# Second mixer of a hybrid decoder trunk: decay and exponential loads with four buffers on ScalarE's queue, decay arithmetic ordered behind the second chunk back

## The chip, the core and the metric

The kernel runs on one core of a Trainium2 chip. A core has five engines that work side by side, each through its own queue in order: TensorE (PE, matmuls and transposes), VectorE (DVE), ScalarE (ACT), GpSimd (POOL) and SyncE (SP, which here only issues loads and stores). They wait for each other by semaphores. Sixteen DMA engines move data between memory (HBM) and the on-chip buffers. The metric is the time of one execution on the device in microseconds (us), as the median of several runs.

## What is computed

A trunk of two layers over 1024 tokens of width 1024, in float32. Layer 0 mixes with an mLSTM and a retention group, layer 1 with a Mamba-2 state-space mixer (SSD); each is followed by a squared-ReLU MLP. The change is in the SSD mixer only. Its core, cut to what matters:

```python
def ssd_chunked(x, dt, a, bm, cm):
    # h_t = exp(dt_t a) h_{t-1} + dt_t x_t B_t^T ;  y_t = h_t C_t, in chunks of 128 tokens
    cs = jnp.cumsum(dt * a.reshape(ng, rep), axis=2)
    seg = jnp.exp(jnp.where(mask, cs[:, :, :, None] - cs[:, :, None, :], -jnp.inf))
    cb = jnp.einsum('bctgn,bcsgn->bctsg', cm, bm)
    m = cb[..., None] * seg * dt[:, :, None]
    y_intra = jnp.einsum('bctsgr,bcsgrp->bctgrp', m, x)
    to_end = jnp.exp(cs[:, :, -1:] - cs) * dt
    states = jnp.einsum('bclgn,bclgr,bclgrp->bcgrpn', bm, to_end, x)
    ...
    y_inter = jnp.einsum('bctgn,bcgrpn->bctgrp', cm, h_prev) * jnp.exp(cs)[..., None]
    return (y_intra + y_inter).reshape(bsz, seq, nh, hp)
```

There are 32 heads in 8 groups of 4 heads; a group shares its B and C (`bm`, `cm`).

## The kernel before

Activations stay on chip for the whole trunk. A projection matrix is kept as a high and a low half (`whi`, `wlo`), and so is the input (`uh`, `ul`); each tile of a projection is a run of 24 matmuls of 128x512 (`proj_in`, L136).

The second mixer is `ssd`. A helper, `ssd_dt`, first works out the cumulated decay `cs` and its exponential `ecs` for all heads and writes both to memory as `cs_d` and `ecs_d`, one row a head. Then a loop over the 8 groups does, for each:

- four projections with two halves of 512 tokens each (B, C, two of x), each followed by a causal convolution: ScalarE copies the product into `xr`, VectorE adds three shifted taps (L784), ScalarE takes a tanh into `th` (L788), VectorE makes the SiLU of it (L789);
- per half, `cb` = C times B for its four chunks (matmuls `cbp`, L811, times a mask, L815);
- per chunk of 128 tokens, the decay tile `cb4` for 4 heads: a load broadcasts a piece of `cs_d` to all 128 partitions (L822), four activations subtract the token's own value (L826, one a head), one takes the exponential (L833), VectorE multiplies it with `cb` (L834);
- in the same chunk on TensorE: three transposes `tr` (L839), the product `yp` within the chunk from `cb4` and `xd` (L848), the product with the carried state (L853), and the new contribution to the state, `ds_`, from `xw` and `bn` (L868). `xd` and `xw` are VectorE's scaled copies of the transposed x (L842, L862); `bn` is ScalarE's plain copy of the transposed B (L866);
- the state update (`sst`: L875 on GpSimd, L880 on VectorE; for chunk 0 the copy L873 on ScalarE), and the output: `eh` (the broadcast `ecs`) times the state product (L882), the skip term (L884) and their sum (L893);
- the gate: two projections `sz` (L903, L904), norm, and the output projection (`proj_out`, L180).

In the trace and in the order, `cb` followed by a number is the tile `cb4`; its loads are written `cb<-cs_d`. In that notation `ds__12166` is a buffer of `ds_` by its number.

The order in which each engine gets its instructions is set by the tile framework's scheduler from the program order and its dependencies; it fills TensorE's queue between the small products of a chunk with matmuls of the following projections (`mmin`, L136). Within an engine nothing overtakes. A tile with `bufs=n` has n buffers in turn, and an instruction that writes a buffer waits until the last reader of its former content is done. `cb4` has two buffers, `eh` one of a whole half, `th` two, `xr` three. Every load is issued by SP (`nc.sync`), in one line with the weights.

Of the kernel before, what the change touches and what calls it, by code (L numbers as in the profile page):

```python
# [7 lines left out]
F32 = mybir.dt.float32  # L8
F32R = mybir.dt.float32r
AF = mybir.ActivationFunctionType  # L10
ALU = mybir.AluOpType

P = 128
# [4 lines left out]
HALF = 512  # L18
# [5 lines left out]
class Trunk:  # L24
# [704 lines left out]
    def ssd(self, w_in, conv_w, conv_b, dt_bias, a_log, d_skip, norm_w, w_out, mask):  # L729
        nc, tc = self.nc, self.tc  # L730
        with ExitStack() as ctx:
            one = ctx.enter_context(tc.tile_pool(name="ss1", bufs=1))
            two = ctx.enter_context(tc.tile_pool(name="ss2", bufs=2))
# [27 lines left out]
            nat, cs_d, ecs_d, dec, by_token = self.ssd_dt(one, w_in, dt_bias, a_log)  # L761


            for g in range(8):
                conv = []
                for j in (2, 3, 0, 1):
                    jt = (g * 2, g * 2 + 1, 16 + g, 24 + g)[j]
                    w = self.split_in(self.load_in(w_in, 2048 + jt * P))
                    outs = []
                    prev = None  # L770
                    for half in range(2):
                        ps = self.proj_in(w, half)
                        t = self.half_tile(half, f"sact{half}")
                        xr = two.tile([P, HALF + 3], F32, name="xr", tag="xr", bufs=3)
                        if half == 0:
                            nc.gpsimd.memset(xr[:, 0:3], 0.0)
                        else:
                            nc.gpsimd.tensor_copy(xr[:, 0:3], prev[:, HALF : HALF + 3])
                        nc.scalar.copy(xr[:, 3 : 3 + HALF], ps)
                        nc.scalar.activation(  # L780
                            t, ps, AF.Identity, scale=cw[:, 3, jt : jt + 1], bias=cw[:, 4, jt : jt + 1]
                        )
                        for k in range(3):
                            nc.vector.scalar_tensor_tensor(  # L784
                                t, xr[:, k : k + HALF], cw[:, k, jt : jt + 1], t, op0=ALU.mult, op1=ALU.add
                            )
                        th = two.tile([P, HALF], F32, name="th", tag="th", bufs=2)
                        nc.scalar.activation(th, t, AF.Tanh)  # L788
                        nc.vector.scalar_tensor_tensor(t, th, 1.0, t, op0=ALU.add, op1=ALU.mult)  # L789
                        outs.append(t)  # L790
                        prev = xr
                    conv.append(outs)
# [3 lines left out]
                hs = slice(g * 4, g * 4 + 4)  # L796
                state = None
                for half in range(2):
                    o = half * HALF
                    eh = two.tile([P, 2, HALF], F32, name="eh", tag="eh", bufs=1)  # L800
                    for tl in range(2):
                        for j in range(2):
                            nc.sync.dma_start(
                                eh[j * 64 : (j + 1) * 64, tl],
                                ecs_d[g * 4 + tl * 2 + j, o : o + HALF].partition_broadcast(64),
                            )

                    cbp = self.sc.tile([P, CPH, P], F32, name="cbp", tag="sc")
                    for cc in range(CPH):
                        s = slice(cc * P, (cc + 1) * P)  # L810
# [3 lines left out]
                    cb = two.tile([P, CPH, P], F32, name="cb", tag="cb", bufs=1)  # L814
                    nc.vector.tensor_mul(cb, cbp, m01.unsqueeze(1).broadcast_to([P, CPH, P]))  # L815
                    y = (x0[half], x1[half])
                    for cc in range(CPH):
                        c = half * CPH + cc
                        s = slice(cc * P, (cc + 1) * P)
                        par, q = c % 2, c // 2  # L820
                        cb4 = two.tile([P, 4, P], F32, name="cb4", tag="cb4", bufs=2)
                        nc.sync.dma_start(  # L822
                            cb4, cs_d[hs, c * P : (c + 1) * P].partition_broadcast(P)
                        )
                        for h in range(4):
                            nc.scalar.activation(  # L826
                                cb4[:, h],
                                cb4[:, h],
                                AF.Relu,
                                scale=-1.0,  # L830
                                bias=nat[:, 2, par, g * 4 + h, q : q + 1],
                            )
                        nc.scalar.activation(cb4, cb4, AF.Exp, scale=-1.0)  # L833
                        nc.vector.tensor_mul(  # L834
                            cb4, cb4, cb[:, cc].unsqueeze(1).broadcast_to([P, 4, P])
                        )
                        tr = self.sc.tile([P, 4, P], F32, name="tr", tag="sc")
                        for j, src in enumerate((x0, x1, bT)):
                            nc.tensor.transpose(tr[:, j], src[half][:, s], self.ident)  # L839
                        xn = tr[:, 0:2].rearrange("p a (h d) -> p (a h) d", h=2)  # L840
                        xd = two.tile([P, 4, 64], F32, name="xd", tag="xd")
                        nc.vector.tensor_mul(  # L842
                            xd, xn, nat[:, 0, par, hs, q : q + 1].broadcast_to([P, 4, 64])
                        )
                        yp = self.sc.tile([P, 4, P], F32, name="yp", tag="sc")
                        for h in range(4):
                            r = slice((h % 2) * 64, (h % 2) * 64 + 64)
                            nc.tensor.matmul(  # L848
                                yp[r, h // 2], xd[:, h], cb4[:, h], start=True, stop=True
                            )  # L850
                        if c > 0:
                            for tl in range(2):
                                nc.tensor.matmul(  # L853
                                    yp[:, 2 + tl],
                                    state[:, tl * P : (tl + 1) * P],
                                    cT[half][:, s],
                                    start=True,
                                    stop=True,
                                )
                        if c < NCH - 1:  # L860
                            xw = two.tile([P, 4, 64], F32, name="xw", tag="xw")
                            nc.vector.tensor_mul(  # L862
                                xw, xn, nat[:, 1, par, hs, q : q + 1].broadcast_to([P, 4, 64])
                            )
                            bn = two.tile([P, P], F32, name="bn", tag="bn")
                            nc.scalar.copy(bn, tr[:, 2])  # L866
                            ds_ = self.sc.tile([P, HALF], F32, name="ds_", tag="sc")
                            nc.tensor.matmul(  # L868
                                ds_[:, 0:256], bn, xw.rearrange("p h d -> p (h d)"), start=True, stop=True
                            )  # L870
                            new = two.tile([P, 256], F32, name="sst", tag="sst")
                            if c == 0:
                                nc.scalar.copy(new, ds_[:, 0:256])  # L873
                            else:
                                nc.gpsimd.tensor_mul(  # L875
                                    new.rearrange("p (h d) -> p h d", h=4),
                                    state.rearrange("p (h d) -> p h d", h=4),
                                    dec[:, hs, c : c + 1].broadcast_to([P, 4, 64]),
                                )
                                nc.vector.tensor_add(new, new, ds_[:, 0:256])  # L880
                        if c > 0:
                            nc.vector.tensor_mul(eh[:, :, s], eh[:, :, s], yp[:, 2:4])  # L882
                        for tl in range(2):
                            nc.vector.scalar_tensor_tensor(  # L884
                                y[tl][:, s],
                                y[tl][:, s],
                                dsk[:, g * 2 + tl : g * 2 + tl + 1],
                                yp[:, tl],
                                op0=ALU.mult,
                                op1=ALU.add,  # L890
                            )
                            if c > 0:
                                nc.vector.tensor_add(y[tl][:, s], y[tl][:, s], eh[:, tl, s])  # L893
                        if c < NCH - 1:
                            state = new
                zs = []
# [214 lines left out]
```

## Time and profile before

| | |
|---|---|
| median of 3 runs | 2788.24 us (2787.37 to 2789.55) |
| the profiled execution, its own time | 2785.3 us |
| its span, first to last instruction | 2783.5 us |
| TensorE busy, share of the span | 2706.2 us, 97% |
| VectorE busy | 1702.9 us, 61% |
| ScalarE busy | 928.1 us, 33% |
| GpSimd busy | 526.6 us, 19% |
| DMA engines, share by the queue of the loads | 19.4% |
| mean granted TensorE clock | 0.993 |

The profile is of one execution. Busy time of TensorE is the time in which a matmul was in its pipeline. The second mixer lies between 1176 and 2085 us of the span.

### The profile page before, as it was taken

Reading aid. Unit: us, or ns where it says so; the run is one execution under the profiler, and the core shown is the slowest. Engines: PE = TensorE matmul, PEld = TensorE weight load, DVE = VectorE, ACT = ScalarE, POOL = GpSimd, SP = SyncE. Lnnn points to the kernel's source line nnn. Section 1 sums busy time; section 2 is a strip of 40 time slices with the busy share of each in tenths; the row PEclk is TensorE's granted clock in tenths of the full one; section 3 lists DMA queues with packets and bytes.
Section 4 is the critical chain, followed back from the end, with each engine's and each line's share of the span. In section 5 each row is a group of like instructions: output and inputs, shape, how many; then the busy total and the mean of one; then the engine's idle time right before and its main releaser. Section 6 shows DMA issues by size and latency. Waiting matters only on the chain.

```text
span 2783.5 us, 32858 instructions
## 1 busy us (share of the span) xinstructions
PE 2706.2 (97%) x12973; PEld 2195.3 (79%) x12973; DVE 1702.9 (61%) x2790; ACT 928.1 (33%) x1515; POOL 526.6 (19%) x526
## 2 busy tenths in 40 slices
PE   8999999999999999899999999999999999999997
PEld 7788788888888888677777787777878888888885
DVE  5663537654466644776766667667676456654457
ACT  5232224222222222453434434344343222222223
POOL 1010111422222322200000000000013222332223
PEclk9999999999999999899999999999999999999998
DMA  4111112110111110132312222222121112110111
GB/s 159 39 62 46 54 54 68 54 41 27 61 61 61 54 38 25 43 84 61 76 51 72 69 61 69 57 72 71 59 54 63 52 61 61 61 38 24 60 38 61
DMA packets 199050, 161.46 MB, mean 58 GB/s; under 512 B 8952, under 2 KB 177840, under 8 KB 198768
## 3 DMA queue, kind: packets, MB, share of 16 engines
q1 hardware_dynamic: 198896, 159.36, 19.4%
q8 instruction: 102, 1.67, 0.2%
q14 instruction: 52, 0.43, 0.1%
HBM read 154.68 MB, written 4.62 MB: 57 GB/s over the span
## 4 chain that ended last, share of the span: by engine, by line
PE 90%; DMA 4%; ACT 2%; DVE 2%; POOL 1%; issue 0%; SPq 0%; DVEq 0%; ACTq 0%; POOLq 0%
PE mmin L136 49%; PE mmout L260 22%; PE mmout L180 9%; DMA cb<-cs_d 4%; PE mmnat L152 3%; PE yp L848 1%; PE pt L223 1%; ACT cb L826 1%; POOL h L355 1%; DVE un L206 1%; PE mmin L162 1%; PE cbp L811 1%; PE av L546 0%; PE tr L839 0%; PE sp L924 0%; PE av L548 0%
## 5 line engine op out<-in xcount | busy, mean ns | idle before, releaser
L136 PE MATMUL mmin<-uh,whi 128*128 128x512 f32 (+1 forms) x2112 | 826.7, 392 | 0.3 <-ACT uh L225 0.3
L136 PE MATMUL mmin<-ul,whi 128*128 128x512 f32 (+1 forms) x2112 | 825.6, 391 | 0.0
L136 PE MATMUL mmin<-uh,wlo 128*128 128x512 f32 (+1 forms) x2112 | 823.5, 390 | 0.0
L136 PEld LDWEIGHTS mmin<-uh,whi 128*128 128x128 f32 x2112 | 397.3, 188 | 89.8 <-issue 1.2
L136 PEld LDWEIGHTS mmin<-uh,wlo 128*128 128x128 f32 x2112 | 397.4, 188 | 88.5 <-issue 0.2
L136 PEld LDWEIGHTS mmin<-ul,whi 128*128 128x128 f32 x2112 | 397.3, 188 | 86.8
L94 DVE TENSOR_TENSOR wlo<-raw,whi 128x1024 fp32r<-128x1024 f32 x240 | 309.6, 1293 | 220.5 <-ACT whi L93 214.0
L93 ACT CAST whi<-raw 128x1024 fp32r<-128x1024 f32 (+1 forms) x243 | 251.1, 1038 | 452.8 <-PE mmin L136 215.3
L260 PE MATMUL mmout<-whi,hl 128*128 128x512 f32 x896 | 353.7, 395 | 0.7 <-DVE hl L94 0.7
L260 PE MATMUL mmout<-wlo,hh 128*128 128x512 f32 x896 | 353.7, 395 | 0.0
L260 PE MATMUL mmout<-whi,hh 128*128 128x512 f32 x896 | 353.6, 395 | 0.0
L180 PE MATMUL mmout<-whi,hid 128*128 128x512 f32 x768 | 245.3, 398 | 0.7 <-ACT hid L610 0.7
L311 DVE TENSOR_TENSOR q<-q 128x512 f32<-128x512 f32 x128 | 95.2, 744 | 222.2 <-ACT q L310 222.2
L283 DVE TENSOR_TENSOR h<-h,mmout 128x512 f32<-128x512 f32 x320 | 208.6, 678 | 33.3 <-PE mmout L260 33.1
L260 PEld LDWEIGHTS mmout<-whi,hl 128*128 128x128 f32 x896 | 168.6, 188 | 41.0 <-DVE hl L94 1.1
L260 PEld LDWEIGHTS mmout<-wlo,hh 128*128 128x128 f32 x896 | 168.6, 188 | 39.9
L260 PEld LDWEIGHTS mmout<-whi,hh 128*128 128x128 f32 x896 | 168.6, 188 | 39.9
L784 DVE SCALAR_TENSOR_TENSOR sact<-xr,cw,sact 128x512 f32<-128x512 f32 x192 | 144.0, 750 | 55.3 <-ACT sact L780 51.4
L180 PEld LDWEIGHTS mmout<-whi,hid 128*128 128x128 f32 x768 | 143.4, 188 | 35.8 <-ACT hid L610 2.4
L310 ACT ACTIVATE q<-mmin 128x512 f32<-128x512 f32 x128 | 76.2, 596 | 269.8 <-PE mmin L136 269.8
L93 ACT CAST hh<-q 128x1024 fp32r<-128x1024 f32 x80 | 84.1, 1051 | 199.0 <-PE mmout L260 110.0
L180 PE MATMUL mmout<-wlo,hid 128*128 128x512 f32 x384 | 150.0, 395 | 0.0
(377 smaller groups left out, 3171.1 us busy)
## 6 DMA issues: line engine op xcount, KB each, us to landing
raw<-in_mlp_w_dram SPq DMA_DIRECT2D x64, 512.0 KB
raw<-in_mlp_w_dram SPq DMA_DIRECT2D x32, 1024.0 KB
raw<-in_ssd_w_in_dram SPq DMA_DIRECT2D x48, 512.0 KB
cb<-cs_d SPq DMA_DIRECT2D x64, 256.0 KB
raw<-in_hyb_w_in_dram SPq DMA_DIRECT2D x24, 512.0 KB
raw<-in_ssd_w_out_dram SPq DMA_DIRECT2D x16, 512.0 KB
eh<-ecs_d SPq DMA_DIRECT2D x64, 128.0 KB
h<-in_x_dram SPq DMA_DIRECT2D x8, 512.0 KB
```

The costliest lines, as they stand in the source:

```text
L93: self.nc.scalar.copy(hi, raw)
L94: self.nc.vector.tensor_sub(lo, raw, hi.bitcast(F32))
L136: self.nc.tensor.matmul(ps[:, o : o + n], a[:, k], u[:, k, s], start=(k == 0 and i == 0), stop=(k == 7 and i == 2),)
L152: self.nc.tensor.matmul(ps, u[:, k, s], a, start=(k == 0 and i == 0), stop=(k == 7 and i == 2))
L162: self.nc.tensor.matmul(ps, w[:, k], u[:, k, s], start=(k == 0 and i == 0), stop=(k == 7 and i == 1))
L180: self.nc.tensor.matmul(ps, a[:, s], w[:, n], start=(kk == 0 and i == 0), stop=(kk == 1 and i == 2))
L206: nc.vector.scalar_tensor_tensor(un[j], self.h[:, c, n], r, wb[j], op0=ALU.mult, op1=ALU.mult)
L260: nc.tensor.matmul(banks[t], a[x][:, kk, s], w[y][:, kk], start=(not more and kk == 0 and i == 0), stop=(not more and kk == 1 and i == 2), ...
L283: nc.vector.tensor_add(y, y, x[t])
L310: nc.scalar.activation(x, ps, AF.Relu)
L311: nc.vector.tensor_mul(x, x, x)
L784: nc.vector.scalar_tensor_tensor(t, xr[:, k : k + HALF], cw[:, k, jt : jt + 1], t, op0=ALU.mult, op1=ALU.add)
```

## The change

The loads of the decay tile go from SP's queue to ScalarE's, with four buffers in place of two. `eh` is loaded per chunk instead of per half: two loads of 64 KB a chunk (none for chunk 0) with four buffers, in place of four loads of 128 KB a half; these too are issued by ScalarE. The activations and the multiply that make the decay tile of a chunk are told to be issued behind two instructions of the second chunk back, its `xw` and its `bn` (`tc.issue_after`; the list `issued` starts empty in each call and runs on over halves and groups, and is an empty entry for the last chunk of a group). The tanh of the convolution writes into the first 512 columns of `xr`, so that `th` needs no memory of its own.

```diff
@@ ssd
+            issued = []
             for g in range(8):
...
-                        th = two.tile([P, HALF], F32, name="th", tag="th", bufs=2)
+                        th = xr[:, 0:HALF]
                         nc.scalar.activation(th, t, AF.Tanh)
...
                 for half in range(2):
-                    o = half * HALF
-                    eh = two.tile([P, 2, HALF], F32, name="eh", tag="eh", bufs=1)
-                    for tl in range(2):
-                        for j in range(2):
-                            nc.sync.dma_start(
-                                eh[j * 64 : (j + 1) * 64, tl],
-                                ecs_d[g * 4 + tl * 2 + j, o : o + HALF].partition_broadcast(64),
-                            )
...
-                        cb4 = two.tile([P, 4, P], F32, name="cb4", tag="cb4", bufs=2)
-                        nc.sync.dma_start(
+                        cb4 = two.tile([P, 4, P], F32, name="cb4", tag="cb4", bufs=4)
+                        nc.scalar.dma_start(
                             cb4, cs_d[hs, c * P : (c + 1) * P].partition_broadcast(P)
                         )
-                        for h in range(4):
-                            nc.scalar.activation(
...
+                        if c > 0:
+                            eh = two.tile([P, 2, P], F32, name="eh", tag="eh", bufs=4)
+                            for j in range(2):
+                                nc.scalar.dma_start(
+                                    eh[j * 64 : (j + 1) * 64],
+                                    ecs_d[hs, c * P : (c + 1) * P]
+                                    .rearrange("(a b) t -> b a t", b=2)[j]
+                                    .partition_broadcast(64),
+                                )
+                        with ExitStack() as order:
+                            for ins in issued[-2] if len(issued) >= 2 else ():
+                                order.enter_context(tc.issue_after(ins))
+                            for h in range(4):
+                                nc.scalar.activation(
+                                    cb4[:, h],
...
+                            nc.scalar.activation(cb4, cb4, AF.Exp, scale=-1.0)
+                            nc.vector.tensor_mul(
...
+                        issued.append([])
                         if c < NCH - 1:
                             xw = two.tile([P, 4, 64], F32, name="xw", tag="xw")
-                            nc.vector.tensor_mul(
+                            xw_ins = nc.vector.tensor_mul(
...
-                            nc.scalar.copy(bn, tr[:, 2])
+                            issued[-1] = [xw_ins.ins, nc.scalar.copy(bn, tr[:, 2]).ins]
...
-                            nc.vector.tensor_mul(eh[:, :, s], eh[:, :, s], yp[:, 2:4])
+                            nc.vector.tensor_mul(eh, eh, yp[:, 2:4])
```

What this makes of ScalarE's queue is seen in the fourth group, from the copy `bn` of chunk 0 on. Before, `cb_12176` and the next numbers are the decay tiles of chunks 2, 3 and 4:

```order
L866 COPY bn<-tr 128x128
L873 COPY sst<-ds__12135 128x256
L903 ACTIVATE sz<-mmin 128x512
L826 ACTIVATE cb_12176<-cb_12176,dnat 128x128
L866 COPY bn<-tr 128x128
L826 ACTIVATE cb_12176<-cb_12176,dnat 128x128 x3
L833 ACTIVATE cb_12176<-cb_12176 128x512
L826 ACTIVATE cb_12211<-cb_12211,dnat 128x128 x4
L866 COPY bn<-tr 128x128
L833 ACTIVATE cb_12211<-cb_12211 128x512
L826 ACTIVATE cb_12258<-cb_12258,dnat 128x128 x4
L866 COPY bn<-tr 128x128
```

The same place of the changed kernel (its lines are higher by some eight; L833 is now the activation of one head, L840 the exponential, L874 the copy `bn`, L816 and L822 the loads of `cb4` and `eh`). `cb_12175` and `cb_12213` are chunks 2 and 3, and `cb_12258`, `cb_12296`, `cb_12334` chunks 4, 5 and 6:

```order
L874 COPY bn<-tr 128x128
L833 ACTIVATE cb_12175<-cb_12175,dnat 128x128 x3
L881 COPY sst<-ds__12131 128x256
L833 ACTIVATE cb_12175<-cb_12175,dnat 128x128
L816 DMA cb_12258<-cs_d 128x4x128
L840 ACTIVATE cb_12175<-cb_12175 128x512
L874 COPY bn<-tr 128x128
L833 ACTIVATE cb_12213<-cb_12213,dnat 128x128 x4
L816 DMA cb_12296<-cs_d 128x4x128
L840 ACTIVATE cb_12213<-cb_12213 128x512
L822 DMA eh<-ecs_d 64x2x128 x2
L874 COPY bn<-tr 128x128
```

Before, the first activation of chunk 2 stood ahead of the copy `bn` of chunk 1, and those of chunk 3 ahead of `bn` of chunk 2. Now the activations of chunk 2 follow `bn` of chunk 0 and those of chunk 3 follow `bn` of chunk 1, and the loads of chunks 4 and 5 and of `eh` stand between them.

On SP's queue, the same group before:

```order
L822 DMA cb_12176<-cs_d 128x4x128
L822 DMA cb_12211<-cs_d 128x4x128
L822 DMA cb_12258<-cs_d 128x4x128
L822 DMA cb_12293<-cs_d 128x4x128
L803 DMA eh<-ecs_d 64x512 x4
L822 DMA cb_12328<-cs_d 128x4x128
L70 DMA raw<-in_ssd_w_in_dram 128x8x128
L822 DMA cb_12363<-cs_d 128x4x128
```

In the changed kernel only the weight loads (`raw`, L70) are left on SP's queue in the groups, eight in a row.

## Rows read from the trace of the kernel before

**Rows 1.** The page's part 4, the chain that ended last, by line.
```profile
PE mmin L136 49%; PE mmout L260 22%; PE mmout L180 9%; DMA cb<-cs_d 4%; PE mmnat L152 3%; PE yp L848 1%; PE pt L223 1%; ACT cb L826 1%; POOL h L355 1%; DVE un L206 1%; PE mmin L162 1%; PE cbp L811 1%; PE av L546 0%; PE tr L839 0%; PE sp L924 0%; PE av L548 0%
```

**Rows 2.** Windows, one a group of the second mixer; the fourth and the sum.
```profile
core 0: us, PE busy (x) PEld busy (x) DVE busy (x) ACT busy (x) POOL busy (x), PEclk, DMA share, GB/s
...
1518.64:1631.43 112.79, 109.13 (x548) 86.69 (x547) 77.18 (x140) 46.10 (x93) 7.42 (x16) 1.00 0.25 66
...
sum 909.06, PE 875.85 PEld 698.11 DVE 629.52 ACT 378.20 POOL 64.03; mean PE 109.48 PEld 87.26 DVE 78.69 ACT 47.27 POOL 8.00
```

**Rows 3.** Waits of PE, 1176 to 2084 us: total us, times, longest us.
```profile
PE yp L848 <- DVE xd L842: 4.1, 7, 1.2
PE ds__10535 L868 <- ACT bn L866: 2.2, 1, 2.2
...
PE ds__15080 L868 <- ACT bn L866: 0.6, 1, 0.6
```

**Rows 4.** Timeline, fourth group: start us, us, instruction [idle before <-releaser].
```profile
1569.69 0.25 ACT L866 COPY bn<-tr 128x128 f32<-128x128 f32 x1
1571.05 0.37 ACT L873 COPY sst<-ds__12135 128x256 f32<-128x256 f32 x1 [1.11 <-PE ds__12135 L868]
1571.85 0.60 ACT L903 ACTIVATE sz<-mmin 128x512 f32<-128x512 f32 x1 [0.42 <-PE mmin L136]
1574.20 0.40 ACT L826 ACTIVATE cb<-cb,dnat 128x128 f32<-128x128 f32 x1 [1.76 <-DMA cb<-cs_d]
1574.51 0.25 ACT L866 COPY bn<-tr 128x128 f32<-128x128 f32 x1
...
1575.68 0.63 ACT L833 ACTIVATE cb<-cb 128x512 f32<-128x512 f32 x1
1577.75 1.28 ACT L826 ACTIVATE cb<-cb,dnat 128x128 f32<-128x128 f32 x4 [1.44 <-DMA cb<-cs_d]
...
1572.79 0.71 PE L853 MATMUL yp<-sact,sst 128*128 128x128 f32 x4
1574.81 0.70 PE L868 MATMUL ds__12166<-xw,bn 128*128 128x256 f32 x2 [1.31 <-ACT bn L866]
...
1578.69 0.71 PE L853 MATMUL yp<-sact,sst 128*128 128x128 f32 x4
1579.24 0.69 PE L868 MATMUL ds__12201<-xw,bn 128*128 128x256 f32 x2
...
1585.16 0.70 PE L868 MATMUL ds__12236<-xw,bn 128*128 128x256 f32 x2 [1.34 <-ACT bn L866]
...
1577.21 0.28 DVE L893 TENSOR_TENSOR sact<-sact,eh 128x128 f32<-128x128 f32 x1
```

**Rows 5.** The chain in order of time, three groups: start us, us, what.
```profile
1364.13 7.08 DMA cb<-cs_d
...
1374.79 3.65 PE mmin L136 x9
...
1569.49 4.69 DMA cb<-cs_d
...
1578.83 4.78 DMA cb<-cs_d
...
1602.11 2.10 PE mmin L136 x9
...
2028.11 3.31 PE mmin L136 x10
```

**Rows 6.** Windows: the chunk stretch of the fourth group, and behind the wait of ds__10535.
```profile
1563.28:1608.45 45.17, 41.51 (x254) 32.09 (x252) 33.70 (x82) 22.92 (x57) 4.12 (x6) 1.00 0.34 81
1374.50:1378.30 3.80, 3.80 (x12) 2.63 (x10) 3.04 (x9) 2.56 (x7) 0.00 (x0) 0.55 0.06 18
```

**Rows 7.** Issues on SP's queue by tile (ns min/median/max).
```profile
L822 SPq DMA_DIRECT2D cb<-cs_d x64: 359/360/522, 1204.6 to 2046.8; - x64
L803 SPq DMA_DIRECT2D eh<-ecs_d x64: 450/592/2141, 1207.9 to 2042.6; - x64
```

More of the change, by code (lines that the diff above doesn't have):

```diff
@@ L820, in ssd @@
                         par, q = c % 2, c // 2
-                        cb4 = two.tile([P, 4, P], F32, name="cb4", tag="cb4", bufs=2)
-                        nc.sync.dma_start(
+                        cb4 = two.tile([P, 4, P], F32, name="cb4", tag="cb4", bufs=4)
+                        nc.scalar.dma_start(
                             cb4, cs_d[hs, c * P : (c + 1) * P].partition_broadcast(P)
                         )
-                        for h in range(4):
-                            nc.scalar.activation(
[L827 to L831, printed above, removed]
-                            )
@@ L833, in ssd @@
-                        nc.scalar.activation(cb4, cb4, AF.Exp, scale=-1.0)
-                        nc.vector.tensor_mul(
-                            cb4, cb4, cb[:, cc].unsqueeze(1).broadcast_to([P, 4, P])
-                        )
+                        if c > 0:
[7 more added lines that the diff above has]
+                                )
@@ new lines, in ssd @@
+                        with ExitStack() as order:
[4 more added lines that the diff above has]
+                                    cb4[:, h],
+                                    cb4[:, h],
+                                    AF.Relu,
+                                    scale=-1.0,
+                                    bias=nat[:, 2, par, g * 4 + h, q : q + 1],
+                                )
+                            nc.scalar.activation(cb4, cb4, AF.Exp, scale=-1.0)
+                            nc.vector.tensor_mul(
+                                cb4, cb4, cb[:, cc].unsqueeze(1).broadcast_to([P, 4, P])
+                            )
@@ L859, in ssd @@
                                 )
+                        issued.append([])
                         if c < NCH - 1:
                             xw = two.tile([P, 4, 64], F32, name="xw", tag="xw")
-                            nc.vector.tensor_mul(
+                            xw_ins = nc.vector.tensor_mul(
                                 xw, xn, nat[:, 1, par, hs, q : q + 1].broadcast_to([P, 4, 64])
@@ L892, in ssd @@
                             if c > 0:
-                                nc.vector.tensor_add(y[tl][:, s], y[tl][:, s], eh[:, tl, s])
+                                nc.vector.tensor_add(y[tl][:, s], y[tl][:, s], eh[:, tl])
                         if c < NCH - 1:
```

## Prediction, made before the changed kernel had run

> **What bounds the kernel now.** I read the page's chain first. TensorE is the bound: its matmuls fill nearly all of the chain that ended last [rows 1]. The largest other entry, 4%, is one kind of load, `cb` from `cs_d`, for the decay tile `cb4` of the second mixer; 1% is ScalarE's work on it. Four per cent of the 2783.5 us span would be 114 us. The reader should not take that as the prize: the chain goes through a load wherever a later product hung on it, also where TensorE had other matmuls to do meanwhile.
>
> So I went next to the view by windows, cut at the eight points where the second mixer starts its long run of projection matmuls, which makes one row for each of its eight groups; the fourth and the sum stand in [rows 2]. In the sum row TensorE is busy 875.85 of 909.06 us: it stands idle **33.2 us**, some 4 us a group. That is the prize, not 114.
>
> The view of waits says on whom [rows 3]. Thirty waits of TensorE fall in this stage, from 1176 to 2084 us. Twenty-three are the state product `ds_` waiting for ScalarE's copy `bn`, from 2.2 down to 0.6 us (the first row and the last); seven are the product `yp` waiting for VectorE's `xd`, 4.1 us together. Why is a 0.25 us copy late? The timeline of the fourth group answers [rows 4]: ScalarE sat 1.76 us in front of the first decay activation of chunk 2, whose load was not there; the copy `bn` of chunk 1 stands behind it in ScalarE's queue, began when the activation had gone, and only then could TensorE do `ds_12166`. The chain by time shows the load itself: issued at 1569.49, when chunk 0's product had freed its buffer, landed 4.69 us later [rows 5]. The next one takes 4.78. With two buffers a load can begin only when the product two chunks earlier is done, and TensorE reaches the place where it is wanted in about the time that it takes.
>
> **The change part by part.**
>
> *Buffers and the issue of the loads.* `cb4` gets four buffers instead of two, and its loads are issued by ScalarE. The order shows that "four chunks ahead" is a number of buffers: the load of chunk c+4 stands behind the first activations of chunk c+2, so two chunks of time lie between it and its use. I walk one case on the fourth group's times. The copy `bn` of chunk 0 starts at 1569.69 [rows 4]; behind it four activations (1.28 us) and the copy `sst` (0.37) let the load of chunk 4 go at about 1571.6. Its activations now stand ahead of `bn` of chunk 3, whose product started at 1585.16, or at 1582.2 with the waits of chunks 1 and 3 gone (1.31 + 0.16 and 1.34 + 0.16, where the 0.16 is explained below). Backing off `bn` (0.25), the `sz` activation (0.60), the exponential (0.63), the four activations (1.28) and two issues of 0.59 leaves 1578.3: **6.7 us of lead**. Loads in this group took 4.69 and 4.78 us; the longest I found in the chain is 7.08 [rows 5]. So the loads are in time but for the longest, which misses by 0.4.
>
> *The decay arithmetic behind bn and xw.* The activations and the multiply of chunk c now stand behind `bn` and `xw` of chunk c-2 in every queue. So even a late load holds up the copies of later chunks only. This costs no instruction.
>
> *What goes.* All 33.2 us of idle time go if each wait goes. To this I add what a wait costs beyond its recorded length. In rows 4 the unwaited `ds_` starts 0.55 us after `yp` L853 (1578.69 to 1579.24), the waited one 2.02 us after (1572.79 to 1574.81) with 1.31 of it recorded: 0.16 more. Thirty times 0.16 is 4.8. Twice the granted clock fell behind a wait: after the 2.2 us wait of `ds_10535` it was 0.55 of full speed, between the levels of 2.4 and 1.2 GHz [rows 6]; nine matmuls took 3.65 us there and 2.10 elsewhere, ten took 3.31, at that rate 2.33 [rows 5]. That is 1.55 + 0.98 = 2.5 us. **Gross: 33.2 + 4.8 + 2.5 = 40.5 us.**
>
> *What ScalarE takes on.* Eight `cb` loads and fourteen `eh` loads a group. Before, all stood on SP's queue, with 0.36 us an issue for `cb` and 0.59 for `eh` (medians), 2.14 at most [rows 7]; no row shows an issue on ScalarE. Between 0 (an issue that hides under an activation still running) and 2.14 I take SP's medians, the same kind of instruction: 8 x 0.36 + 14 x 0.59 = 11.1 us. In the chunk stretch of a group ScalarE is busy 22.9 us of 45.2, and TensorE's work there is 41.5 [rows 6]. 22.9 + 11.1 = 34.0 fits under 41.5, so the issues cost nothing by sum. By place it is tighter. The two `eh` issues ahead of `bn` of chunk 2 wait for VectorE's last add of chunk 1 (it ends at 1577.49 [rows 4]). Two issues end at 1578.67, and `bn` may start as late as 1578.94 (1579.24 less 0.25 and the 0.05 between them). The margin is 0.27 us, and for an issue of more than 0.72 us it is gone. TensorE, through `ds_`, is who waits then.
>
> *VectorE, SP and the rest.* `eh` is now loaded a chunk at a time, same bytes, so VectorE's instructions stay the same in number and shape; it is busy 33.7 of 41.5 us in the stretch [rows 6]. SP loses the 128 issues; weight loads no longer stand behind loads that wait for a buffer. The view of waits names no weight that TensorE waits for, so that is worth nothing. A few issues on ScalarE wait for the semaphore of a weight load as well; by the order that load was issued ten microseconds of matmuls and more before, so I price it at zero. The tanh that now writes into `xr` holds that buffer until VectorE's last use; three buffers stand against 5.6 us of matmuls a tile (24, at 2.10 us for nine), so zero too.
>
> *The sum.* Against 40.5 I set one new wait of 1 us a group, 8 us, for margins as thin as 0.27 and for the waits on VectorE, which the change does not address. Net -32.5. The profiled execution took 2785.3 us, its span 2783.5 and 1.8 around it, and lands at 2752.8. The median of the three runs is 2.9 above it: **2755.7 us**. The lower end is the gross gain kept whole, 2747.7, and 1.7 of margin.
>
> **The page that speaks against it.** From issue to landing a load of `cb` took 4.69 and 4.78 us from SP's queue, and the DMA engines were busy 0.34 of the stretch [rows 5, 6]. The Trainium skill, "DMA: Bandwidth & Descriptors", section "Issuing engines are not separate DMA queues", says that transfers from all issuing engines share the same 16 engines and interleave, so that a second issuing engine saves only issue time. By that rule the move to ScalarE's queue alone would leave the time at 2788; the sum above credits nothing to it, only to the earlier issue, and the rule stands behind the first rival.
>
> **The rivals.**
>
> *Loads land later than now.* `cb`, `eh` and weights are no longer in one line, so more are under way at once. For it: the one load of 7.08 us. Against it: engines busy a third of the time. If a load takes 8.2 us instead of 4.7, it is 1.5 us late; at two chunks a group that keeps 2 x 8 x 1.47 = 23.5 us of the waits. 40.5 - 23.5 = 17: **2771 us**.
>
> *VectorE takes over the wait.* Its queue is in order, and a product with `yp` stands ahead of the next `xd`. For it: seven of the thirty waits are `yp` on `xd` already, and VectorE is 81% busy against TensorE's 41.5. Against: those seven are 4.1 us together, and where no load was late `yp` got `xd` in time. If it took all of the time back, no change: **2788 us**.
>
> *The issue blocks ScalarE: slower.* Each of the 22 issues a group occupies ScalarE for d. Once 22.9 + 22 d exceeds the 45.2 us that the stretch takes now, ScalarE is the bound: **from d = 1.01 us on**. At 1.2 us it is 49.3, 4.1 us a group, 33 in all: **2821 us**. For it: SP's issues up to 2.14. Against: their medians, 0.36 and 0.59.
>
> **How the numbers follow.** Forecast 0.60, loads later 0.18, VectorE 0.08, issue blocks 0.12, and 0.02 for a gain beyond the range. A measurement of this kernel tells 0.2%, 5.6 us, from no change. Faster by more than that are the forecast, the later loads and the 0.02: 0.80; same 0.08; slower 0.12. The range takes in the forecast and the later loads with some margin: 2746 to 2778.
>
> **What would show it.** Right: the windows by group give TensorE 1 us or less idle, groups of 108 to 110 us; the `ds_` waits vanish from the waits; ScalarE's waits for `cs_d` all but vanish, below 20 us in all; the clock stays at full through the groups. Wrong: `ds_` waits for `bn` behind an issue on ScalarE's queue, or `cb` from `cs_d` still on the chain, or `yp` waiting for `xd` more than 10 us in all.

## The result, and the profile after

| | before | changed |
|---|---|---|
| median | 2788.51 us (4 runs, 2787.37 to 2789.55) | 2748.89 us (4 runs, 2748.43 to 2750.98) |
| ratio, 95% interval | | 0.9859 (0.9842 to 0.9877) |
| profiled execution: time, span | 2785.3, 2783.5 us | 2750.98, 2749.2 us |
| TensorE busy | 2706.2 us | 2700.5 us, 98% |

The change made the kernel faster by 39.6 us between the medians; the two profiled spans differ by 34.3. Each set of runs below has runs of the kernel before on the same chip, so kernels of different sets are compared through their ratios.

The windows by group, the answer to [rows 2]: the first seven groups of the changed kernel. The cuts are the starts of its own groups but for the first, 1176.07, which is taken over from the kernel before.

```profile
core 0: us, PE busy (x) PEld busy (x) DVE busy (x) ACT busy (x) POOL busy (x), PEclk, DMA share, GB/s
1176.07:1294.41 118.34, 113.84 (x610) 92.55 (x609) 84.16 (x169) 51.67 (x109) 9.24 (x16) 0.97 0.33 82
1294.41:1402.53 108.12, 108.12 (x547) 86.62 (x547) 77.47 (x140) 46.15 (x93) 7.04 (x16) 1.00 0.30 67
...
1510.76:1619.05 108.29, 108.29 (x548) 86.68 (x547) 77.55 (x140) 46.15 (x93) 7.04 (x16) 1.00 0.27 68
...
sum 767.36, PE 762.82 PEld 612.26 DVE 549.02 ACT 328.62 POOL 51.47; mean PE 108.97 PEld 87.47 DVE 78.43 ACT 46.95 POOL 7.35
```

From the second group on TensorE does not stand still: 108.12 us of work in 108.12 us, where the fourth group of before had 109.13 in 112.79 [rows 2]. The first group is the exception: 4.5 us idle. Its 118.34 us are not all its own: this execution came to the group's start at 1179.87, 3.8 us behind the cut.

The waits of TensorE in these groups, which answer to [rows 3], and what is left of ScalarE's waits for `cs_d` (120.8 us in 54 waits before):

```profile
PE tr L846 <- DVE sact L791: 4.5, 1, 4.5
```
```profile
ACT sz L911 <- DMA cb<-cs_d: 2.6, 1, 2.6
```

All thirty waits of `ds_` for `bn` and `yp` for `xd` are gone. One new one has come, in the first group. The chain's lines [rows 1] now read as follows; the load of `cb` has left them:

```profile
PE mmin L136 50%; PE mmout L260 22%; PE mmout L180 9%; PE mmnat L152 3%; PE yp L855 1%; PE yp L860 1%; PE pt L223 1%; POOL h L355 1%; PE tr L846 1%; DVE un L206 1%; PE av L546 0%; PE cbp L805 0%; PE mmin L162 0%; PE av L548 0%; PE sp L932 0%; PE sco L516 0%
```

The lead can be read off ScalarE's timeline of the fourth group. The loads of chunks 4, 5 and 6 are issued at 1563.17, 1565.01 and 1569.67, and their first activations start at 1569.69, 1572.97 and 1578.18, none of them after a wait for data:

```profile
1563.17 0.37 ACTq L816 DMA_DIRECT2D cb<-cs_d  x1
...
1565.01 0.37 ACTq L816 DMA_DIRECT2D cb<-cs_d  x1
...
1569.67 0.38 ACTq L816 DMA_DIRECT2D cb<-cs_d  x1
1569.69 1.28 ACT L833 ACTIVATE cb<-cb,dnat 128x128 f32<-128x128 f32 x4
...
1572.97 1.28 ACT L833 ACTIVATE cb<-cb,dnat 128x128 f32<-128x128 f32 x4
...
1578.18 1.28 ACT L833 ACTIVATE cb<-cb,dnat 128x128 f32<-128x128 f32 x4
```

That is 6.5, 8.0 and 8.5 us; over six loads of this stretch (chunks 4 to 7, and chunks 0 and 1 of the next group) it runs from 5.9 to 8.5.

The new wait is a matter of start-up. In the first group all buffers are free, and twelve loads stand in ScalarE's queue in the middle of the convolution. ScalarE's timeline there:

```profile
1209.80 0.37 ACTq L816 DMA_DIRECT2D cb<-cs_d  x1
1210.26 4.67 ACTq L822 DMA_DIRECT2D eh<-ecs_d  x2
...
1215.77 0.63 ACT L790 ACTIVATE xr<-sact 128x512 f32<-128x512 f32 x1 [5.37 <-issue]
...
1222.35 0.63 ACT L790 ACTIVATE xr<-sact 128x512 f32<-128x512 f32 x1 [4.78 <-issue]
```

ScalarE stands idle 5.37 and 4.78 us in front of two tanh activations (L790), behind issues. Not all of that is the time of an issue: in the chain in order of time the `eh` issue of 1220.98, just ahead of the second tanh, stands behind the landing of an earlier `cb` load, 11.16 us after that load's own issue.

```profile
1209.80 11.16 DMA cb<-cs_d
1220.98 0.58 ACTq L822
```

The delay runs through VectorE's taps to the transposes:

```profile
1229.88 0.69 PE L846 MATMUL tr<-ident,sact 128*128 128x128 f32 x2 [4.50 <-DVE sact L791]
...
1231.22 0.63 PE L136 MATMUL mmin<-uh,wlo 128*128 128x512 f32 x1
```

Behind the wait, from 1230.2 to 1234.2, the granted clock was 0.50, the lower of the two levels, 1.2 GHz.

### The profile page after: what moved, and what is told of

Read it like the earlier page. It is cut to its first block, busy times and chain, and to the rows that moved or that the text cites. A ratio compares the mean times of both kernels' runs of the same rounds, so it can differ in the third digit from the quotient of the medians.

```text
span 2749.2 us, 32841 instructions
## 1 busy us (share of the span) xinstructions
PE 2700.5 (98%) x12973; PEld 2195.6 (80%) x12973; DVE 1706.2 (62%) x2790; ACT 928.1 (34%) x1515; POOL 526.1 (19%) x526
## 4 chain that ended last, share of the span: by engine, by line
PE 94%; DVE 3%; POOL 1%; DMA 1%; ACT 1%; issue 0%; SPq 0%; ACTq 0%; DVEq 0%; POOLq 0%
PE mmin L136 50%; PE mmout L260 22%; PE mmout L180 9%; PE mmnat L152 3%; PE yp L855 1%; PE yp L860 1%; PE pt L223 1%; POOL h L355 1%; PE tr L846 1%; DVE un L206 1%; PE av L546 0%; PE cbp L805 0%; PE mmin L162 0%; PE av L548 0%; PE sp L932 0%; PE sco L516 0%
## 5 line engine op out<-in xcount | busy, mean ns | idle before, releaser
L283 DVE TENSOR_TENSOR h<-h,mmout 128x512 f32<-128x512 f32 x320 | 208.8, 679 | 32.7 <-PE mmout L260 32.5
```

The lines of the kernel that those rows point to most:

```text
L283: nc.vector.tensor_add(y, y, x[t])
```

## The experiments

The theory at first: the lead of the loads is what pays, and it comes from the two more buffers. The rivals: the ordering pays, or the queue does.

**Fewer buffers.** Everything else of the change is kept.

```diff
-                        cb4 = two.tile([P, 4, P], F32, name="cb4", tag="cb4", bufs=4)
+                        cb4 = two.tile([P, 4, P], F32, name="cb4", tag="cb4", bufs=2)
```

> The changed kernel with two buffers for the decay tile cb4 instead of four; loads still on ScalarE's queue, decay arithmetic still ordered behind bn and xw of the second chunk back. Theory (the lead of the loads did it): a load can again go only when the product two chunks earlier is done, so TensorE's idle time in the second mixer comes back, 25 to 40 us of it, and the time is 2775 to 2795; the waits may now be of yp for cb4 and not of ds_ for bn, since bn no longer stands behind the late activations. Rival (the order of the arithmetic did it: with bn ahead, a late load costs little): 2750 to 2765.

2788.16 us, ratio 1.0002 (0.9992 to 1.0011): the whole gain is gone.

> The changed kernel with three buffers for cb4 instead of four; queue and ordering as in the change. With four, the loads of the fourth group stood 5.9 to 8.5 us ahead of their activations; a chunk takes TensorE some 4 to 5 us there, so three leave 2 to 4 us, against loads that take 4.7. Theory (the lead decides, a chunk of it per buffer): some waits come back but fewer than with two, 2755 to 2780. Rival (once the order is kept, one spare buffer is enough, and the fourth is worth nothing): 2747 to 2751.

2763.45 us, ratio 0.9908 (0.9891 to 0.9924). The time that ScalarE waited in front of the first decay activation (L833) gives the series. With two buffers, and with three:

```profile
  DMA cb<-cs_d: 105.8, 59
```
```profile
  DMA cb<-cs_d: 73.1, 40
```

With four there was none. TensorE's waits of `ds_` and `yp` follow: 29.9 us in 39 waits with two buffers, 7.2 in 12 with three, none with four. Each buffer takes away a part of the waits, as the theory has it. The waits with two are partly of `yp` for `cb4`, as expected: 16 of them, 8.1 us.

**Buffers without the order, the order without buffers.** First the kernel before with four buffers and nothing else (the tanh goes into `xr`, for room):

```diff
-                        th = two.tile([P, HALF], F32, name="th", tag="th", bufs=2)
+                        th = xr[:, 0:HALF]
-                        cb4 = two.tile([P, 4, P], F32, name="cb4", tag="cb4", bufs=2)
+                        cb4 = two.tile([P, 4, P], F32, name="cb4", tag="cb4", bufs=4)
```

> The kernel before with only four buffers for cb4 (the tanh written into xr to make the room, as in the change); loads on SP's queue, eh in half-row loads into one buffer as before, no ordering. Theory (lead alone): the waits of ds_ for bn go, and SP takes the issues, so ScalarE has no late tanh in the first group: 2741 to 2752. Rival (the order is needed too, because an activation that waits still holds bn): 2760 to 2780. Rival (SP's queue is in line behind weight loads, so the earlier free buffer does not bring an earlier load): 2775 to 2788.

2823.13 us, ratio 1.0133 (1.0118 to 1.0147): slower than before, which no theory had. ScalarE's order in the fourth group says why. `cb_12226` and `cb_12261` are chunks 4 and 5 here:

```
L873 COPY sst<-ds__12103 128x256
L903 ACTIVATE sz<-mmin 128x512
L826 ACTIVATE cb_12226<-cb_12226,dnat 128x128
L866 COPY bn<-tr 128x128
L826 ACTIVATE cb_12226<-cb_12226,dnat 128x128 x3
L833 ACTIVATE cb_12226<-cb_12226 128x512
L826 ACTIVATE cb_12261<-cb_12261,dnat 128x128 x4
L866 COPY bn<-tr 128x128
```

With two buffers the activations of chunk 2 stood ahead of `bn` of chunk 1. With four, those of chunk 4 stand there. The scheduler moved the arithmetic two chunks ahead along with its load, so the time from load to use did not grow. ScalarE's timeline:

```profile
1590.58 0.40 ACT L826 ACTIVATE cb<-cb,dnat 128x128 f32<-128x128 f32 x1 [1.78 <-DMA cb<-cs_d]
1590.88 0.24 ACT L866 COPY bn<-tr 128x128 f32<-128x128 f32 x1
```

and the chain in order of time there:

```profile
1585.22 0.61 PE yp L848 x8
...
1585.85 4.71 DMA cb<-cs_d
...
1591.18 0.70 PE ds__12134 L868 x2
```

It is the picture of [rows 4], wait for wait: the load goes when chunk 0's product has freed its buffer, and `bn` of chunk 1 stands behind its first activation. Now it costs more, because at a group's end the activations of the next group stand ahead of the norm's square (L913): TensorE waited 32.7 us in `ds_` and 18.3 in `sp`, the sum of squares, 51.0 against the 33.2 of before. The rest of the loss was not taken apart; the mean granted clock of the profiled execution was 0.987, against 0.993 before.

Then the changed kernel without its ordering:

```diff
-                            for ins in issued[-2] if len(issued) >= 2 else ():
+                            for ins in ():
```

> The changed kernel without the ordering of the decay arithmetic behind bn and xw. Theory (with the loads in time nothing waits at the head of ScalarE's queue, so the order is worth nothing): 2746 to 2754. Rival (the order is half of it): 2760 to 2775, with ds_ waiting for bn again.

2797.97 us, ratio 1.0039 (1.0025 to 1.0052): not only half of it, all of it. The chain shows the same pattern on ScalarE's queue:

```profile
1577.05 5.46 DMA cb<-cs_d
1582.51 0.03 issue
1582.54 1.29 ACT cb L833 x4
...
1584.62 0.27 ACT bn L874
...
1584.93 0.70 PE ds__12241 L876 x2
```

The ordering alone, put on the kernel before, was not run: with two buffers the scheduler's order is then that of the kernel before on every engine, row for row. The constraint bites only where there are buffers to run ahead into.

So the first theory fell in its simple form. A new one: buffers and order make the lead together; the one lets the load go early, the other keeps its use late. The queue is worth nothing.

**The queue.** The changed kernel with SP issuing:

```diff
-                        nc.scalar.dma_start(
+                        nc.sync.dma_start(
                             cb4, cs_d[hs, c * P : (c + 1) * P].partition_broadcast(P)
...
-                                nc.scalar.dma_start(
+                                nc.sync.dma_start(
                                     eh[j * 64 : (j + 1) * 64],
```

> The changed kernel with the cb4 and eh loads issued by SP instead of ScalarE, all else kept. Theory (lead alone; all issuing engines feed the same DMA engines): no loss in groups 2 to 8, and the first group's late tanh (4.5 us of TensorE and a fallen clock behind it) goes: 2741 to 2749. Rival (ScalarE's queue is what lets the loads go early, SP's being blocked by other waits): 2765 to 2788.

2768.67 us, ratio 0.9937 (0.9924 to 0.9949): half the gain is lost, as the rival had it, but not by its mechanism. TensorE has just seven waits in the groups, one in each but the last; the longest:

```profile
PE ds__15098 L876 <- ACT bn L874: 2.6, 1, 2.6
```

In the fourth group it is the last `bn` of the group, behind an activation of the next group's second chunk, whose load had only been issued at 1585.33. In the chain:

```profile
1584.67 0.61 PE yp L855 x8
...
1585.33 5.30 DMA cb<-cs_d
...
1591.90 0.70 PE ds__12362 L876 x2
...
1592.93 3.65 PE mmin L136 x9
```

The change orders that chunk behind an empty list, since the last chunk of a group has no `bn`. On ScalarE's queue the scheduler happened to keep the order there (closing the place in the changed kernel moves no row of ScalarE's queue); on SP's it did not. With the place closed, on top of the edit above:

```diff
-                        issued.append([])
+                        issued.append(issued[-1] if c == NCH - 1 else [])
```

> The run with the loads on SP's queue, and one place in the ordering closed: the decay arithmetic of a group's second chunk, which the change orders behind an empty list (the last chunk before it has no bn), is ordered behind bn and xw of the last chunk that has one. In the run on SP's queue each of seven groups had one wait of ds_ for bn, 1.9 to 2.6 us, behind an activation of the next group's second chunk whose load had just been issued. Theory (the arithmetic standing ahead of bn is what costs, the queue that issues is worth nothing): the seven waits go, 15.3 us and the 1.5 us of slow clock behind each, and the first group has no late tanh: 2741 to 2748. Rival (SP's queue in order delays the loads behind eh loads that wait for a buffer): the waits move to another chunk, 2760 to 2769.

2742.79 us, ratio 0.9844 (0.9830 to 0.9857). All seven waits are gone; the first group has none in either run. The two ratios lie 25.9 us apart. In the two profiles the windows from one group's first `cbp` matmul to the next group's, seven of them, show where it went; the fourth, the fifth and the sum with the place open, and the sum with it closed:

```profile
1558.41:1670.25 111.84, 109.94 (x548) 87.50 (x547) 77.20 (x140) 45.99 (x93) 7.02 (x16) 0.98 0.27 65
1670.25:1780.91 110.66, 108.38 (x547) 86.51 (x546) 77.22 (x140) 45.99 (x93) 7.02 (x16) 1.00 0.27 66
...
sum 781.78, PE 766.45 PEld 611.41 DVE 541.39 ACT 325.18 POOL 48.80; mean PE 109.49 PEld 87.34 DVE 77.34 ACT 46.45 POOL 6.97
```
```profile
sum 756.78, PE 756.78 PEld 605.12 DVE 541.15 ACT 326.66 POOL 48.90; mean PE 108.11 PEld 86.45 DVE 77.31 ACT 46.67 POOL 6.99
```

The difference is 25.0 us, of which 15.3 are recorded waits. In five of the seven groups the clock fell behind the wait, as in the fourth (0.98 in its window, 109.94 us of work); in the third and the fifth it stayed full (1.00, 108.38). That is 1.56 us a group, 7.8 in five. The 1.9 us that are left, 0.27 a wait, are what a wait costs beyond its recorded length.

So the queue gains nothing: 0.9844 here with SP, and 0.9844 further down with ScalarE from the second group on. The Trainium skill, "DMA: Bandwidth & Descriptors", section "Issuing engines are not separate DMA queues", says just this: transfers from all issuing engines share the same 16 engines, and another issuer saves issue time only. The two equal ratios agree.

**The smallest form.** The kernel before with four buffers and the ordering (closed), loads on SP and `eh` by half rows as before; to the diff of the buffers alone comes

```diff
+                        with ExitStack() as order:
+                            for ins in issued[-2] if len(issued) >= 2 else ():
+                                order.enter_context(tc.issue_after(ins))
...
+                        issued.append(issued[-1] if c == NCH - 1 else [])
```

> The kernel before with four buffers for cb4 (tanh into xr) and the ordering of the decay arithmetic (with the empty place closed), and nothing else: loads on SP's queue, eh in half-row loads as before. Four buffers alone gave 2823, because the arithmetic moved ahead of bn along with its load. Theory (buffers and order together make the lead; queue and the split of eh are worth nothing): 2741 to 2750, 73 to 82 us below four buffers alone. Rival (the half-row eh load waits for its one buffer and holds the cb4 loads behind it on SP's queue): one wait a group, 2755 to 2772. Rival (the order is not the cause of the 35 us lost by four buffers alone): 2800 or more.

2743.38 us, ratio 0.9845 (0.9832 to 0.9858), 79.7 us below the four buffers without the order. Every group from the second on took 108.1 us. Splitting `eh` by chunk and moving the loads to ScalarE's queue add nothing to these two edits: the whole change, with its late first group, lies at 0.9859.

> The kernel before with four buffers and the ordering as the change has it, with the empty place behind a group's last chunk left open; loads on SP's queue, eh in half-row loads. Closed, it gave 2743. In the order the activations of the next group's second chunk now stand ahead of the last bn of a group again. Theory (that place alone costs one wait of about 2 us and a fallen clock behind it in seven groups): 2760 to 2770. Rival (the place matters only together with the eh loads a chunk): 2741 to 2748.

2755.88 us, ratio 0.9900 (0.9884 to 0.9917), between the theory's 2760 and the rival's 2748 and nearer to the theory: the seven waits are there, but of 1.2 to 1.8 us. The chain in the fourth group shows what I had counted and did not come:

```profile
1579.43 4.76 DMA cb<-cs_d
...
1586.42 0.70 PE ds__12321 L873 x2
...
1587.44 2.10 PE mmin L136 x9
```

Nine matmuls behind the wait take 2.10 us, not 3.65, and so they do behind all seven: the clock did not fall. The same seven windows:

```profile
sum 768.32, PE 758.73 PEld 605.63 DVE 538.34 ACT 326.70 POOL 48.94; mean PE 108.39 PEld 86.52 DVE 76.91 ACT 46.67 POOL 6.99
```

With the place closed they again sum to 756.78, 11.5 us less: 9.7 of recorded waits and about 0.27 a wait beyond them.

**The first group.** Loads of the first group on SP, of the others on ScalarE:

```diff
-                        nc.scalar.dma_start(
+                        (nc.sync if g == 0 else nc.scalar).dma_start(
```

(at both loads).

> The changed kernel, with the loads of the first of the eight groups issued by SP and those of the other seven by ScalarE. Theory (in the first group the issues on ScalarE's queue, one of them 3.57 us, hold the tanh back, and TensorE waits 4.5 us for it with the clock falling behind): the wait goes and the time is 2741 to 2746. Rival (the tanh is late because cs_d itself is written late, whoever issues): 2748 to 2751.

2741.62 us, ratio 0.9844 (0.9830 to 0.9857). The windows from the first group's first `cbp` matmul to the second group's, in the changed kernel and in this one, and this one's second group:

```profile
1224.21:1339.05 114.84, 110.34 (x548) 88.14 (x547) 82.22 (x148) 51.82 (x107) 7.27 (x18) 0.97 0.26 70
```
```profile
1221.28:1329.43 108.15, 108.15 (x548) 86.61 (x547) 78.23 (x143) 49.19 (x103) 7.09 (x16) 1.00 0.30 76
```
```profile
1284.79:1392.91 108.12, 108.12 (x547) 86.60 (x547) 77.47 (x140) 46.16 (x93) 7.04 (x16) 1.00 0.28 68
```

The late tanh cost 6.7 us (114.84 against 108.15), 4.5 of them idle and the rest behind the wait, with its lower clock; and it was the loads on ScalarE's queue that made it late. The 9.6 us of the next expectation come from windows cut at the fixed time 1176.07 (118.34 and 108.72). They hold 2.9 us by which the two executions differed earlier, at that first matmul (1224.21 and 1221.28); two executions of this one kernel differ as much (1221.28 and 1223.99). Since the ratios of this kernel and of the changed one came from two chips, both were run once more side by side.

> The changed kernel itself, beside the next run on the same chip. Its first result came from another chip than the run with the first group's loads on SP, and the two ratios to the kernel before (0.9859 and 0.9844) have overlapping intervals, although the first group's windows differ by 9.6 us (118.34 and 108.72). Theory (the first group's late tanh costs the whole kernel its 9.6 us): a ratio of 0.985 to 0.987, 5 to 10 us above the next run. Rival (the chips differ, the wait is made up later): within 2 us of it.

> The changed kernel with the first group's loads on SP, on the same chip as the changed kernel. Theory: 5 to 10 us below it, 0.982 to 0.984 of the kernel before. Rival: within 2 us of it.

2749.66 us (2748.16 to 2750.02), ratio 0.9874 (0.9860 to 0.9889), against 2743.73 (2741.62 to 2744.39), ratio 0.9853 (0.9838 to 0.9868). The difference is 5.9 us in the medians, in the expected range, and no run of one lies among those of the other; the ratios lie 0.0004 and 0.0013 above the ranges expected of them. In the two profiles the stretch of the first group, cut as above, took 114.67 and 108.14 us, 6.5 apart.

**More issues on ScalarE.** Each chunk's `eh` in four loads:

```diff
-                                    eh[j * 64 : (j + 1) * 64],
-                                    ecs_d[hs, c * P : (c + 1) * P]
...
+                                for tl in range(2):
+                                    nc.scalar.dma_start(
+                                        eh[j * 64 : (j + 1) * 64, tl],
```

> The changed kernel with each chunk's eh brought in by four loads instead of two, same bytes: 14 more issues a group on ScalarE, 8 us at the 0.58 us of an eh issue. Theory (an issue stands beside a running activation and ScalarE is far from full): 2747 to 2755. Rival (the margin of 0.27 us that the prediction found for the copy bn behind two eh issues decides): ds_ waits for bn about 0.9 us at two or more chunks a group, 2763 to 2785.

2753.47 us, ratio 0.9882 (0.9869 to 0.9896), above the changed kernel's 0.9859 and 0.9874 but with overlapping intervals. No `ds_` waits for `bn`: the theory holds for the chunks. What the issues cost shows in another place, in TensorE's waits and in ScalarE's timeline behind the last chunks:

```profile
PE mmout L180 <- ACT hid L927: 3.1, 7, 0.9
```
```profile
1601.62 5.42 ACTq L823 DMA_DIRECT2D eh<-ecs_d  x5
1607.09 0.72 ACT L927 ACTIVATE hid<-sz,snw 128x512 fp32r<-128x512 f32 x1 [8.07 <-DMA cb<-cs_d]
```

Eleven issues stand in a row there, from 1598.01 to 1607.04 (a `cb`, four `eh`, a `cb` and the five `eh` shown), and ScalarE stands idle 8.07 us before the gate's `hid`, behind them. TensorE waits for `hid` 0.9 us at most.

## Why the prediction was right, and where it was wrong

**The time.** 2755.7 was forecast, 2748.89 measured, inside the range. Between the profiled executions the forecast was -32.5 us and the spans show -34.3. The other 5.0 us of the miss are how those executions lie to their medians: the forecast put the median 2.9 us above the profiled execution, and it came out 2.1 below. That -32.5 came so near is in part luck. By the next two paragraphs the gain was 3.6 us larger than forecast and the new wait 1.3 smaller; against that, the profiled execution of the changed kernel came to the mixer's first `cbp` matmul 3.5 us later than that of before (1224.21 against 1220.73), ahead of the new wait, as executions of one kernel also differ.

**What bounds the kernel** was read rightly: the idle time of the windows was the prize, and not the chain's 4%. The waits named went, all thirty.

**The gross gain** was mis-sized a little. With no wait and the clock full, a group takes 108.12 us (the second of the run with the first group on SP), eight of them 864.96. Against 909.06 [rows 2] that is 44.1 us, not 40.5. The term that was too small is what a wait costs beyond its recorded length: 0.27 us by the two kernels with seven waits, not 0.16, which makes 8.1 us for thirty waits in place of 4.8. The three kernels without any wait were 43.2 to 45.0 under the kernel before, and 41.1 on the last chip.

**"One new wait of 1 us a group = 8 us"** had about the right size and the wrong shape. Seven groups have none. The first has one, 6.7 us with the fallen clock. The prediction added up ScalarE's issues over the chunk stretch and looked for their margin there; it did not ask what the first loads of all, which wait for no buffer, would stand in front of. That place was in the order. It also priced at zero what issues on ScalarE wait for earlier loads, thinking of weights; in the first group one waited for the `cb` load of 11.16 us.

**"The loads are in time: 6.7 us of lead"**: right, 5.9 to 8.5. But the prediction took the lead for a gift of the buffers and of the earlier issue, and the ordering for something that costs no instruction and holds up later chunks only. That is the step that failed, and the sum does not show it, since the change has both. Buffers alone lose 34.8 us; the change without the order loses 9.6.

**The queue priced at nothing**: right from the second group on. Issues on ScalarE took 0.37 us for `cb` and 0.58 for `eh`, as SP's did [rows 7]:

```profile
L816 ACTq DMA_DIRECT2D cb<-cs_d x64: 366/367/691, 1207.9 to 2006.9; - x64
```
```profile
L822 ACTq DMA_DIRECT2D eh<-ecs_d x112: 581/582/3572, 1210.3 to 2009.4; - x112
```

**The margin of 0.27 us** at `bn` of chunk 2 never decided anything: with twice the `eh` issues no `ds_` waited. The issues that hurt stand elsewhere, at the start and at a group's end.

**The tanh in `xr`, the weights on SP** at zero: right. Groups of 108.1 us have both. Weight loads on SP did wait for `cb` loads (70.3 us in all), and TensorE for no weight.

**The rivals.** Loads did not land too late for their lead: no decay activation of the changed kernel waited for one. They could take longer than the 4.7 and 4.8 us of the fourth group before [rows 5], as that rival had it: where the chain of the run without the ordering shows one it took 4.6 to 6.6 us, and 11.6 at the first group's start. VectorE took over no wait. The issues on ScalarE made TensorE wait once, at start-up.

## What to carry to other kernels

An early load gains nothing unless its use stays late: with more buffers a scheduler may move the use ahead along with the load, so look in the order at what stands between the two, and give buffers and an ordering together. The Trainium skill, "DMA: Bandwidth & Descriptors", section "Rules for kernel authors", has both halves: issue early, compute, wait late. The runs agree: early issue alone took 2823.13 us, both halves 2743.38. And before loads go onto an engine that also computes, look at what stands behind the first ones of all, which wait for no buffer.

## What the runs showed that had not been expected

An issue on ScalarE's queue does not wait for the activations ahead of it to end. In the order of the changed kernel's fourth group the load at 1569.67 stands behind the four activations that begin at 1569.69 (for 1.28 us, in the timeline above); its issue is over at 1570.05, beside them. It is the instructions behind an issue that pay: `eh` issues in a row took up to 3.57 us for one at the first group's start. That nothing overtakes within an engine, as told of the kernel before, has this exception.

The clock did not fall behind every wait. After the fourth group's wait of 1.4 us in the run with the ordering's place left open the granted clock was 1.00 (nine matmuls in 2.10 us), after the 1.9 us wait of the same group with the loads on SP it was 0.54, nearly all at the lower level of 1.2 GHz (3.65 us). But the length of the wait does not decide alone: in that second kernel the fifth group's wait was 2.3 us long, and the clock behind it was 1.00. The three windows, and that wait:

```profile
1587.40:1589.60 2.20, 2.20 (x12) 1.51 (x12) 2.20 (x8) 1.26 (x3) 0.00 (x0) 1.00 0.19 46
```
```profile
1592.90:1596.60 3.70, 3.70 (x12) 2.45 (x12) 3.27 (x8) 1.94 (x5) 0.00 (x0) 0.54 0.32 55
```
```profile
1705.10:1707.30 2.20, 2.20 (x12) 1.51 (x12) 2.20 (x8) 1.95 (x5) 0.00 (x0) 1.00 0.39 57
```
```profile
1704.11 0.70 PE L876 MATMUL ds__13274<-xw,bn 128*128 128x256 f32 x2 [2.28 <-ACT bn L874]
```

What else decides is not shown by these runs. Seven such waits lengthened the groups by 25.0 us in one kernel and 11.5 in the other: 5.6 us of the difference are longer waits, 7.8 the clock that fell behind five of the seven.
